# Second block of a fused network: a norm's residual rows in pieces on VectorE beside the next product, and the transposes of log f placed behind the products of q

## The chip, the cores and the metric

One core of a Trainium2 chip runs the whole program in one launch. The metric is device microseconds of that core. Before the change, three runs gave a median of 2824.99 us (2821.97 to 2828.13).

## The reference, cut to what matters

Two networks run one after the other on 256 tokens of width 1024, each with two layers. The first (an RWKV mixer with convolutions) ends in an RMS norm with the gain `final_g`. The second, which the change touches, is, per layer,

```python
x = layer_norm(ALPHA * x + 0.5 * swiglu_2(x, ffn1_w13[l], ffn1_w2[l]), ln_g[l, 0], ln_b[l, 0])
m = mixer(x, ...)
x = layer_norm(ALPHA * x + m, ln_g[l, 1], ln_b[l, 1])
x = layer_norm(ALPHA * x + 0.5 * swiglu_2(x, ffn2_w13[l], ffn2_w2[l]), ln_g[l, 2], ln_b[l, 2])
```

The mixer multiplies x by one wide matrix, whose parts are called q, f, i, g, u, v, a and b. From f it makes a gate and `log_f`, whose running sums give the decays of a recurrence (HGRN2); q reads the state of that recurrence. Everything is float32.

## The kernel before, in words

**Products.** Each float32 product is three matmuls: a weight tile of 128x1024 is split into a high half `wh` (a cast on ScalarE, L339) and a low half `wl` (raw minus high, on VectorE, L340), the moving operand likewise, and `mm3` adds high*high, high*low and low*high (L331). `stream` brings the tiles in order: a transfer by the SP queue into one of four `raw` buffers (L346), then the split into one of five slots for each half (second block). `up` makes one feature tile from eight such steps.

**Norms.** `ln` first adds the product's result to ALPHA*x (L1143), half by half, and takes its statistics; `ln_norm` writes the normalised rows `yb`. Then `feature_major` transposes `yb` on TensorE (L436), and ScalarE, VectorE and GpSimd take the result out of PSUM in a written-out order (`EVAC`), with gain and bias applied per feature: a scaled tile (L452 to L456), its high half (L458) and its low half (L460). That is `xf`, the operand of the next product. The first weight tiles behind it are held: the low halves of two of them are made on GpSimd (L363), the following ones on VectorE behind the last evacuation.

The next norm also needs the normalised rows times gain plus bias in row form, as its residual. So behind `feature_major` two rows come in by transfers (L1168), and GpSimd runs for each of the two row blocks a multiplication (L1162) and an addition (L1163) of 128x1024 each. There are five such norms in the second block: three in layer 0 and two in layer 1, whose third takes another path, straight to the output. And there is one more place, at the head of `second`, where the final RMS norm of the first network has a gain but no bias (L1536).

**The mixer's head.** `mixer` takes four weight tiles for f (`mf`), applies sigmoids (L1184, L1186), a scaling on VectorE (L1187 to L1189) and a logarithm (L1191, function Ln). Then `log f` is transposed on TensorE (L1196) into two PSUM tiles of the lane that the products use, and ScalarE copies them out (L1198). After that come the four tiles for q, copied out by L1204, and then, in the next stage, eight tiles `mt` for i and v. The transposed log f is first read in the stage after that, where `E` tiles of decays are made (L1243 on).

**What sets the order.** The program is traced in Python; a scheduler then simulates a timeline and orders each engine's instructions by program position among those that are ready, so an instruction may be moved ahead of earlier ones that still wait. `issue_after` adds an edge to the order of one engine. `tick` advances a background generator `self.bg` by one step: `ffn` calls it once for each of its 22 feature tiles. In the second block that generator is empty before the change.

Of the kernel before, what the change touches and what calls it, by code (L numbers as in the profile page):

```python
# [14 lines left out]
P = 128  # L15
# [14 lines left out]
NRAW, NW, NL = 4, 3, 2  # L30
NW2, NL2 = 2, 3
NFIRST = 2

NLAST = 2, 4

# [221 lines left out]
class Prog:  # L257
# [75 lines left out]
    def mm3(self, out, w, x, start, stop):  # L333
        self.mm(out, w[0], x[0], start, False)
        self.mm(out, w[0], x[1], False, False)
        self.mm(out, w[1], x[0], False, stop)

    def split(self, src, hi, lo):
        self.nc.scalar.copy(hi, src)  # L339
# [183 lines left out]
    def up(self, out, w, x, n=NF):  # L523

        for k in range(n):
            s = slice(k * P, k * P + P)
            self.mm3(out, (w[0][:, s], w[1][:, s]), x[k], k == 0, k == n - 1)

    def accs(self):
        return [[self.pacc(2 * b + h) for h in range(2)] for b in range(2)]  # L530
# [606 lines left out]
    def ln(self, x, acc, l, i):  # L1137

        nc = self.nc

        def pre(b, h):
            s = HALF[h]
            nc.vector.scalar_tensor_tensor(x[b][:, s], x[b][:, s], ALPHA, acc[b][h], ALU.mult, ALU.add)  # L1143

        g, bt = l * 3 + i, 6 + l * 3 + i
        if l == 1 and i == 2:
            gr, br = self.row(g), self.row(bt)
            for b in range(2):
                y = self.ln_norm(x[b], b, pre)
                for h in range(2):  # L1150
                    e = nc.vector if h == b else nc.gpsimd
                    e.tensor_mul(y[:, HALF[h]], y[:, HALF[h]], gr[:, HALF[h]])  # L1152
                    e.tensor_add(y[:, HALF[h]], y[:, HALF[h]], br[:, HALF[h]])  # L1153
                    nc.sync.dma_start(self.ap["out"][b * P : b * P + P, HALF[h]], y[:, HALF[h]])
            return None
        go, bo = COLS[f"lng{l}"][0] + i * 8, COLS[f"lnb{l}"][0] + i * 8
        yb = [self.ln_norm(x[b], b, pre) for b in range(2)]
        xf = self.feature_major(yb, lambda f: self.cols[:, go + f : go + f + 1],
                                lambda f: self.cols[:, bo + f : bo + f + 1])
        gr, br = self.row(g), self.row(bt)  # L1160
        for b in range(2):
            nc.gpsimd.tensor_mul(x[b], yb[b], gr)  # L1162
            nc.gpsimd.tensor_add(x[b], x[b], br)  # L1163
        return xf

    def row(self, i):
        r = self.S([P, D])
# [3 lines left out]
    def mixer(self, l, xf):  # L1171
# [17 lines left out]
                nc.vector.tensor_scalar(lf[:, h, :], sg, 1e-19, None, ALU.max)  # L1189
        for h2 in range(2):  # L1190
            nc.scalar.activation(lf[:, 2 * h2 : 2 * h2 + 2, :], lf[:, 2 * h2 : 2 * h2 + 2, :], AF.Ln)  # L1191
        lft = []
        for b in range(2):
            pt = self.ps((P, 4, P))
            for h in range(4):
                nc.tensor.transpose(pt[:, h, :], lf[:, h, b * P : b * P + P], self.cst("ident"))  # L1196
            t = self.T2([P, 4, P])
            nc.scalar.copy(t, pt)  # L1198
            lft.append(t)
        for h2 in range(2):  # L1200
            pu = self.ps((P, 2, T))
            for j in range(2):
                self.up(pu[:, j, :], next(st), xf)
            nc.scalar.copy(qs[:, 2 * h2 : 2 * h2 + 2, :], pu)  # L1204
        yield

        st = self.stream(f"mt{l}")
        it, vt = self.S([P, 2, 512]), self.S([P, 2, 512])
        for part in range(2):
            pb = [self.ps() for _ in range(2)]  # L1210
            for k2 in range(4):
                w = next(st)
                for kk in range(2):
                    k = k2 * 2 + kk
                    ws = [w[i][:, kk * 512 : kk * 512 + 512] for i in range(2)]
                    for b in range(2):
                        s = slice(b * P, b * P + P)
                        for a, c in ((0, 0), (0, 1), (1, 0)):
                            self.mm(pb[b], xf[k][a][:, s], ws[c], k == 0 and a == 0 and c == 0, k == 7 and a == 1)
            for b in range(2):  # L1220
                if part == 0:
                    nc.scalar.copy(it[:, b, :], pb[b])
                else:
                    nc.scalar.activation(vt[:, b, :], pb[b], AF.Gelu_apprx_tanh)
# [305 lines left out]
    def second(self):  # L1530
        nc = self.nc

        xf = self.feature_major(self.x, lambda f: self.col("fg", f), None)
        gr = self.row(12)
        for b in range(2):
            nc.gpsimd.tensor_mul(self.x[b], self.x[b], gr)  # L1536
        nc.sync.dma_start(self.h4T, self.ap["h4T"])
        mf = self.S([P, 7 * P])
        nc.sync.dma_start(mf, self.ap["msk"])
        nc.vector.tensor_copy(self.msk, mf)  # L1540
        nc.sync.dma_start(self.ind, self.ap["ind"])
        self.triu = self.ind[:, 8 * P : 9 * P]
        for l in range(2):
            acc = self.ffn(xf, f"pu{l}", f"pd{l}", 0.5)
            xf = self.ln(self.x, acc, l, 0)
            for _ in self.mixer(l, xf):
                pass
            acc = self.wout(self.mixed, f"mo{l}")
            xf = self.ln(self.x, acc, l, 1)
            acc = self.ffn(xf, f"qu{l}", f"qd{l}", 0.5)  # L1550
            xf = self.ln(self.x, acc, l, 2)
# [72 lines left out]
```

## Time and profile before

| | |
|---|---|
| median of 3 runs | 2824.99 us (2821.97 to 2828.13) |
| profiled execution, own time | 2827.67 us |
| its span | 2825.4 us, 53790 instructions |
| TensorE matmul (PE) busy | 2654.2 us, 94% |
| VectorE (DVE) busy | 1740.3 us, 62% |
| ScalarE (ACT) busy | 1332.7 us, 47% |
| GpSimd (POOL) busy | 734.4 us, 26% |
| second block | from about 1570 us to the end |

PE is the engine that matters: its matmuls fill nearly the whole span, so time goes where PE waits, or where its granted clock (PEclk, 1.00 is 2.4 GHz, 0.50 is 1.2 GHz) is at the lower level. The times in a timeline are microseconds from the start of the span; "idle before" names what the engine waited for.

### The profile page before, as it was taken

The numbers are of one execution on the slowest core, as the hardware profiler recorded it, in microseconds if no ns is written. First come the engines' busy times: TensorE is split into PE (matmuls) and PEld (weight loads), VectorE is DVE, ScalarE is ACT, GpSimd is POOL, SyncE is SP. The second block draws the span as 40 slices with busy tenths as digits, with TensorE's granted clock in tenths as the row PEclk, the third lists the DMA queues.
The fourth block names the chain that finished last, engine by engine and source line by source line (L and its number), as shares of the span: only waits on it lengthen the run. The fifth ranks groups of instructions, "written<-read, shape, count | busy, mean of one in ns | idle before, by whom it ended". The sixth has DMA issues, their size and how long they took to land. (4 is left out here: it accounts for less than half of the span.)

```text
span 2825.4 us, 53790 instructions
## 1 busy us (share of the span) xinstructions
PE 2654.2 (94%) x22398; PEld 2308.0 (82%) x22398; DVE 1740.3 (62%) x2659; ACT 1332.7 (47%) x2019; POOL 734.4 (26%) x691
## 2 busy tenths in 40 slices
PE   7889989999889998899899899899999999899998
PEld 4866867888578896766799899789899898789897
DVE  3875778654586556974555655665655655656655
ACT  5523654434564346433544544644444544644443
POOL 0387999920130002483100100200200201200200
PEclk8979999999999999979899999999999999999999
DMA  6344425334223453243455554524555554425553
GB/s 246 108 143 166 151 83 179 132 124 176 93 89 114 142 186 120 100 165 108 149 185 187 187 187 172 175 83 161 170 185 178 179 187 164 154 89 179 194 187 120
DMA packets 118768, 430.70 MB, mean 152 GB/s; under 512 B 13175, under 2 KB 13687, under 8 KB 118525
## 3 DMA queue, kind: packets, MB, share of 16 engines
q1 hardware_dynamic: 118524, 427.28, 43.6%
q8 instruction: 175, 2.87, 0.4%
q14 instruction: 69, 0.56, 0.1%
HBM read 425.13 MB, written 2.10 MB: 151 GB/s over the span
## 5 line engine op out<-in xcount | busy, mean ns | idle before, releaser
L340 DVE TENSOR_TENSOR wl<-raw,wh 128x1024 fp32r<-128x1024 f32 (+1 forms) x654 | 851.6, 1305 | 635.0 <-ACT wh L339 403.2
L339 ACT CAST wh<-raw 128x1024 fp32r<-128x1024 f32 (+1 forms) x654 | 682.3, 1046 | 902.1 <-PE pb L331 356.9
L331 PE MATMUL pb<-S,wh 128*128 128x256 f32 x2560 | 496.3, 291 | 7.6 <-DVE S L460 4.8
L331 PE MATMUL pb<-xf,wh 128*128 128x256 f32 (+1 forms) x2560 | 489.1, 290 | 12.9 <-DVE T1b L585 4.3
L331 PEld LDWEIGHTS pb<-xf,wh 128*128 128x128 f32 (+1 forms) x2560 | 412.5, 195 | 26.7 <-DVE T1b L585 7.8
L331 PEld LDWEIGHTS pb<-S,wh 128*128 128x128 f32 x2560 | 412.5, 194 | 24.5 <-issue 11.4
L331 PE MATMUL ps<-S,wh 128*128 128x256 f32 x2048 | 396.6, 290 | 5.2 <-DVE S L460 3.0
L363 POOL TENSOR_TENSOR wl<-raw,wh 128x1024 fp32r<-128x1024 f32 x22 | 54.8, 2499 | 1325.7 <-ACT wh L362 934.5
L331 PE MATMUL pb<-xf,wl 128*128 128x256 f32 (+1 forms) x1280 | 373.4, 292 | 8.9 <-DVE wl L340 8.9
L331 PE MATMUL pb<-S,wl 128*128 128x256 f32 x1280 | 370.0, 289 | 2.9 <-DVE wl L340 2.9
L331 PEld LDWEIGHTS ps<-S,wh 128*128 128x128 f32 x2048 | 331.9, 195 | 15.6 <-DVE S L460 4.3
L331 PE MATMUL ps<-S,wl 128*128 128x256 f32 x1024 | 296.3, 289 | 4.5 <-DVE wl L340 4.5
L331 PEld LDWEIGHTS pb<-xf,wl 128*128 128x128 f32 (+1 forms) x1280 | 250.3, 196 | 17.1 <-DVE wl L340 11.9
L331 PEld LDWEIGHTS pb<-S,wl 128*128 128x128 f32 x1280 | 248.0, 194 | 7.9 <-DVE wl L340 3.7
L331 PE MATMUL acc<-wh,T 128*128 128x512 f32 x704 | 206.4, 394 | 1.5 <-ACT T L339 1.5
L331 PEld LDWEIGHTS ps<-S,wl 128*128 128x128 f32 x1024 | 199.2, 195 | 6.8 <-DVE wl L340 4.9
L331 PE MATMUL acc<-wh,T1b 128*128 128x512 f32 x528 | 158.8, 399 | 3.5 <-ACT T1b L339 3.5
L729 POOL TENSOR_SCALAR tap<-z,cols 128x255 f32<-128x255 f32 (+14 forms) x120 | 154.6, 1297 | 0.0
L331 PEld LDWEIGHTS acc<-wh,T 128*128 128x128 f32 x704 | 127.3, 189 | 26.0 <-ACT T L339 1.9
L729 POOL TENSOR_SCALAR tap<-x,cols 128x246 f32<-128x246 f32 (+6 forms) x104 | 111.5, 1080 | 45.6 <-DVE x L668 45.5
L730 POOL TENSOR_TENSOR x<-x,tap 128x247 f32<-128x247 f32 (+8 forms) x132 | 105.3, 797 | 38.4 <-ACT tap L727 32.1
L331 PE MATMUL acc<-wl,T 128*128 128x512 f32 x352 | 113.2, 395 | 0.0
(448 smaller groups left out, 4025.5 us busy)
## 6 DMA issues: line engine op xcount, KB each, us to landing
raw<-in_fu SPq DMA_DIRECT2D x132, 512.0 KB, 3.2
raw<-in_ada SPq DMA_DIRECT2D x96, 512.0 KB, 4.1
raw<-in_pu SPq DMA_DIRECT2D x88, 512.0 KB, 3.9
raw<-in_qu SPq DMA_DIRECT2D x88, 512.0 KB, 4.2
raw<-in_fd SPq DMA_DIRECT2D x66, 512.0 KB, 3.2
raw<-in_wr SPq DMA_DIRECT2D x51, 512.0 KB, 3.6
raw<-in_pd SPq DMA_DIRECT2D x44, 512.0 KB, 3.5
raw<-in_qd SPq DMA_DIRECT2D x44, 512.0 KB, 3.6
```

Source lines behind the costliest of these rows:

```text
L331: return self.nc.tensor.matmul(out, lhsT, rhs, start=start, stop=stop, **kw)
L339: self.nc.scalar.copy(hi, src)
L340: self.nc.vector.tensor_sub(lo, src, hi.bitcast(F32))
L363: self.nc.gpsimd.tensor_sub(lo, r, hi.bitcast(F32))
L729: nc.gpsimd.tensor_scalar(t[:, d], z[:, f, s], w(j), None, ALU.mult)
L730: nc.gpsimd.tensor_add(zc[f][:, d], zc[f][:, d], t[:, d])
```

## The change

It has two parts. The residual rows leave GpSimd: a generator `affine` makes them on VectorE in pieces of 128x512, one per `tick`, after three empty ticks; `ffn` ticks once per feature tile, and the mixer's `mt` stage now ticks twice for each of its eight weight tiles. And the transposes of log f stand behind the last matmul of q, with PSUM tiles of another lane ("h", the four accumulator banks).

```diff
+NLATE = 3
...
     def mm3(self, out, w, x, start, stop):
...
-        self.mm(out, w[1], x[0], False, stop)
+        return self.mm(out, w[1], x[0], False, stop)
...
-        gr, br = self.row(g), self.row(bt)
-        for b in range(2):
-            nc.gpsimd.tensor_mul(x[b], yb[b], gr)
-            nc.gpsimd.tensor_add(x[b], x[b], br)
+        self.bg = self.affine(x, yb, self.row(g), self.row(bt))
         return xf
+
+    def affine(self, x, y, g, b=None):
+        nc = self.nc
+        for _ in range(NLATE):
+            yield
+        for i in range(2):
+            for s in HALF:
+                nc.vector.tensor_mul(x[i][:, s], y[i][:, s], g[:, s])
+                if b is not None:
+                    yield
+                    nc.vector.tensor_add(x[i][:, s], x[i][:, s], b[:, s])
+                yield
...
-        lft = []
-        for b in range(2):
-            pt = self.ps((P, 4, P))
-            for h in range(4):
-                nc.tensor.transpose(pt[:, h, :], lf[:, h, b * P : b * P + P], self.cst("ident"))
-            t = self.T2([P, 4, P])
-            nc.scalar.copy(t, pt)
-            lft.append(t)
         for h2 in range(2):
             pu = self.ps((P, 2, T))
             for j in range(2):
-                self.up(pu[:, j, :], next(st), xf)
+                last = self.up(pu[:, j, :], next(st), xf)
             nc.scalar.copy(qs[:, 2 * h2 : 2 * h2 + 2, :], pu)
+        lft = []
+        with self.tc.issue_after(last.ins):
+            for b in range(2):
+                pt = self.ps((P, 4, P), "h")
+                for h in range(4):
+                    nc.tensor.transpose(pt[:, h, :], lf[:, h, b * P : b * P + P], self.cst("ident"))
+                t = self.T2([P, 4, P])
+                nc.scalar.copy(t, pt)
+                lft.append(t)
         yield
...
             for k2 in range(4):
+                self.tick()
+                self.tick()
                 w = next(st)
...
-        gr = self.row(12)
-        for b in range(2):
-            nc.gpsimd.tensor_mul(self.x[b], self.x[b], gr)
+        self.bg = self.affine(self.x, self.x, self.row(12))
```

## Rows read from the trace of the kernel before

**Rows 1.** Busy time by stretch: feed-forward, then `mt`; PE, PEld, DVE, ACT, POOL, PEclk, DMA
```profile
1600.00:1755.00 155.00, 155.00 (x1111) 146.35 (x1110) 79.82 (x93) 68.57 (x93) 0.00 (x0) 1.00 0.56 190
...
1805.00:1828.00 23.00, 23.00 (x100) 18.39 (x99) 11.00 (x10) 12.43 (x15) 0.00 (x0) 1.00 0.54 186
```

**Rows 2.** Waits of PE in the second block (1570 to 2825): total us, times, longest
```profile
PE acc L436 <- DVE S L404: 8.2, 5, 1.6
...
PE ps L331 <- DVE wl L340: 4.5, 2, 2.3
PE pb L1196 <- ACT S L1191: 3.9, 1, 3.9
PE ps L331 <- DVE S L460: 3.0, 2, 1.8
PE pb L331 <- DVE S L460: 2.9, 2, 1.8
PE pb L331 <- DVE wl L340: 2.9, 3, 2.3
PE ps L1196 <- ACT S L1191: 2.7, 1, 2.7
PE acc L331 <- ACT T L339: 1.5, 2, 1.3
```

**Rows 3.** POOL's groups by line, the whole span: count, busy us, mean ns
```profile
L1163 POOL TENSOR_TENSOR x<-x,S 128x1024 f32<-128x1024 f32 x10 | 33.5, 3368 | 0.0
...
L1162 POOL TENSOR_TENSOR x<-S,S 128x1024 f32<-128x1024 f32 x10 | 25.4, 2562 | 0.0
```

**Rows 4.** POOL's timeline at the first norm of layer 0: start, us
```profile
1775.11 5.07 POOL L1162 TENSOR_TENSOR x<-S,S 128x1024 f32<-128x1024 f32 x2
```

**Rows 5.** DVE's timeline at the same norm and behind it
```profile
1771.95 1.10 DVE L460 TENSOR_TENSOR S<-T,S 128x256 fp32r<-128x256 f32 x3
...
1774.68 3.27 DVE L460 TENSOR_TENSOR S<-T,S 128x256 fp32r<-128x256 f32 x2 [0.72 <-ACT S L458]
1777.88 11.19 DVE L340 TENSOR_TENSOR wl<-raw,wh 128x1024 fp32r<-128x1024 f32 x4
...
1790.36 1.21 DVE L340 TENSOR_TENSOR wl<-raw,wh 128x1024 fp32r<-128x1024 f32 x1
...
1805.63 0.69 DVE L1311 TENSOR_TENSOR T<-T,ind 128x512 f32<-128x512 f32 x1 [1.23 <-DMA T<-in_sgws]
```

**Rows 6.** Busy time and granted clock in short stretches at the five norms (columns as in rows 1)
```profile
1771.00:1776.00 5.00, 4.07 (x22) 3.06 (x22) 4.20 (x9) 4.91 (x13) 2.31 (x3) 1.00 0.50 185
1778.00:1783.80 5.80, 5.79 (x27) 5.79 (x28) 5.80 (x2) 2.33 (x2) 5.80 (x3) 0.50 0.26 85
2007.70:2012.80 5.10, 5.10 (x24) 5.10 (x25) 5.10 (x2) 0.26 (x1) 5.10 (x2) 0.50 0.47 157
2197.10:2200.40 3.30, 3.30 (x18) 3.30 (x18) 2.55 (x7) 3.24 (x10) 1.42 (x2) 0.51 0.50 187
2207.30:2210.80 3.50, 3.50 (x19) 3.50 (x18) 3.50 (x2) 0.88 (x1) 3.50 (x2) 0.51 0.45 150
2394.90:2398.50 3.60, 3.53 (x14) 3.15 (x15) 2.86 (x8) 3.50 (x10) 1.01 (x2) 0.53 0.62 245
2401.90:2405.40 3.50, 3.50 (x17) 3.50 (x18) 3.50 (x2) 2.33 (x2) 3.50 (x2) 0.51 0.00 0
2416.30:2419.00 2.70, 2.70 (x13) 2.70 (x14) 1.73 (x3) 2.67 (x4) 0.00 (x0) 0.50 0.78 228
2630.70:2634.00 3.30, 3.30 (x18) 3.30 (x16) 3.30 (x2) 0.00 (x0) 3.30 (x2) 0.50 0.46 166
```

**Rows 7.** PE's timeline at that norm: the last matmul of f
```profile
1789.53 0.28 PE L331 MATMUL pb<-S,wl 128*128 128x256 f32 x1
```

**Rows 8.** ACT's timeline there: the second logarithm
```profile
1798.32 0.63 ACT L1191 ACTIVATE S<-S 128x512 f32<-128x512 f32 x1
```

**Rows 9.** SP's queue at that norm: when the two rows are asked for
```profile
1768.53 0.90 SPq L1168 DMA_DIRECT2D S<-in_rows  x2
```

More of the change, by code (lines that the diff above doesn't have):

```diff
@@ L526, in up @@
             s = slice(k * P, k * P + P)
-            self.mm3(out, (w[0][:, s], w[1][:, s]), x[k], k == 0, k == n - 1)
+            last = self.mm3(out, (w[0][:, s], w[1][:, s]), x[k], k == 0, k == n - 1)
+        return last
     def accs(self):
```

## The prediction

> **What bounds the kernel now.** I read the busy time by stretch first. In the feed-forward parts and in the mixer's `mt` stage PE is busy for the whole stretch, at the full granted clock, while DVE is busy 79.8 of 155 us and 11.0 of 23 us [rows 1]. So in these stages PE sets the pace and DVE has about half of its time free. What can be won or lost lies where PE waits, and I read the list of its waits next [rows 2]. There I see four kinds that bear on the change: for the last evacuations of a norm (`S L460`), for low halves of weights (`wl L340`), for log f (`S L1191`), and for a product's own halves (`T L339`).
>
> The timelines say why the first two are late. POOL begins its four row operations at 1775.11 [rows 4], with means of 2.56 and 3.37 us for the multiplication and the addition [rows 3]: 2 x 2.56 + 2 x 3.37 = 11.9 us, so to about 1787. DVE needs 1.10 us for three evacuations before that, 0.37 each; the last two take 3.27 us together, and then four weight splits take 11.19 us, 2.80 each, where one after POOL's end takes 1.21 [rows 5]. Both engines read two SBUF operands; while they run together DVE is slowed more than twofold. The reader is to see that POOL's work, which nothing waits for, sits at the one place in which DVE is PE's supplier.
>
> The third thing is the clock. Right behind these gaps the granted clock is at 0.50 for 5.8, 5.1, 3.5, 3.5 and 3.3 us, at all five norms, and for 2.7 us behind the longer wait for log f [rows 6].
>
> **The change part by part.** The sum goes against the profiled execution, 2827.67 us for a span of 2825.4; that is 2.7 us above the median, so I take the gain off the median, 2824.99.
>
> *POOL's rows gone.* DVE then makes the last two evacuations in 2 x 0.37 = 0.7 us in place of 3.27, and each split in 1.21 in place of 2.80 [rows 5]. At the first norm the last evacuation would come at 1774.68 + 0.74 = 1775.4 instead of 1777.95; PE stood still from about 1776.2 (its wait of 1.8 us ends at 1778.0 [rows 2, 6]), so the wait goes, with 0.8 us to spare. The first DVE-made weight would be ready at 1776.6. It is wanted when the first two weights are through: 27 matmuls were still to run at 1778.0 [rows 6], 3.1 us at the full rate from 1776.2, so at 1779.3: 2.7 us to spare. The waits that go are 3.0 + 2.9 us for evacuations (four) and 4.5 + 2.9 us for low halves (five), 13.3 us; the 1.5 us for a product's halves go too, since they queue on DVE behind the same splits [rows 2]. Sum 14.8 us.
>
> *The clock behind those gaps.* At 0.50, 27 matmuls of 256 columns took 5.8 us, 0.215 each [rows 6]; in the `mt` stage 100 of 512 columns took 23 us, 0.115 for 256 [rows 1]. So 1 - 0.115 / 0.215 = 46% of a slow stretch is lost: 0.46 x (5.8 + 5.1 + 3.5 + 3.5 + 3.3) = 9.8 us, if the clock no longer falls.
>
> It may still fall. The norm leaves gaps of its own (`S L404`, 8.2 us in five waits [rows 2]), and at two norms the clock was low before POOL's work mattered, from 2197.1 and from 2394.9; at the first norm it was full between 1771 and 1776, so there these gaps had not lowered it [rows 6]. From the two in five I expect about one further fall: 0.46 x 3.3 = 1.5 us given back. At worst all three norms that were spared fall, 4.6 us. The Trainium skill, "TensorE: Matmul & The Clock Gate", part 1 (the HAM clock gate), says that the gate watches activity in windows that run free of the kernel, so the same gap may lower the clock in one place and not in another. By that rule the two in five are a matter of phase and are drawn anew after the change; with all three falling the sum would be 3 us lower than mine. The trace agrees so far as like norms differ.
>
> *The transposes.* PE waits 3.9 and 2.7 us for log f at the head of the two mixers [rows 2], and the stretch of 2.7 us at the low clock behind the longer one costs 0.46 x 2.7 = 1.2 us: together 7.8 us. With q's products next, PE goes straight on: its weights lie ready, since their splits follow the four of the 11.19 us, which shrink to 4.8. The eight transposes take the same PE time wherever they stand. What is late next is log f itself: its second logarithm ends 9.2 us after PE's last matmul of f (1798.95 against 1789.8 [rows 7, 8]); q's four tiles are 4 x 24 matmuls of 0.115, 11.0 us. So the transposes find it ready with 1.8 us to spare, and a miss would cost little more than a microsecond in each mixer; if the cover were wholly gone, it would be the old 6.6 us. The copies out of PSUM stay on ACT, twice per mixer, and their reader is a whole stage of 23 us away. The PSUM lane "h" is empty then, as the norm's evacuation is over. I take the gain of 7.8 whole.
>
> *The pieces on DVE.* Five norms with 8 pieces and one with 4 make 44. The nearest row is a 128x512 product of two SBUF tiles, 0.69 us [rows 5]: 44 x 0.69 = 30.4 us of DVE. In the feed-forward part one comes per tile, and DVE is half idle; in `mt` eight come in about 12 us beside splits of 1.21 per 2.9 us, which raises DVE from 48% to (11.0 + 5.5) / 23 = 72%. The cover is this idle time and the split slots ahead of PE, so the price is nothing as long as the pieces lie there. But the scheduler moves ready work forward: a mixer constant that the program asks for two stages later was made at 1805.63, in the middle of q's and `mt`'s work [rows 5]. A piece may so slip in between evacuations or splits, where it costs 0.69 less the slack worked out above. Bounds: 0, and 8 x 0.69 = 5.5 us a norm; I take 0.5 us at each of the six places, 3.0 in all, nearer to nothing because of the slack of 0.8 and 2.7 us.
>
> *The other queues.* SP asks for the same two rows at the same point (1768.53 [rows 9]), and they had landed when POOL began at 1775.11 [rows 4]; no transfer is added. DVE, not POOL, now waits for them: behind it queue the splits. POOL has nothing behind its rows before the next norm.
>
> Sum: 14.8 + 9.8 + 7.8 - 1.5 - 3.0 = 27.9 us; 2824.99 - 27.9 = 2797.1.
>
> **The rivals.** *A: the clock goes on falling at every norm*, because the norm's own gaps suffice. For it: 2197.1 and 2394.9. Against: the full clock at the first norm. If each fall were as long as now, the 9.8 us stay, the 1.5 of my forecast is counted in them: 14.8 + 7.8 - 3.0 = 19.6, giving 2805.4.
>
> *B: the pieces slip ahead of the splits.* All eight before the first low half cost 5.5 - 2.7 = 2.8 us at each of five norms, 14 us, and the gaps so made lower the clock as now: 9.8 - 1.5 = 8.3 more than I allow. 27.9 + 3.0 - 14 - 8.3 = 8.6, giving 2816.4. For it: the early constant. Against: three empty ticks, and splits stand earlier in the program.
>
> *C: slower.* A piece stands in DVE's queue ahead of the evacuations and waits there for its row. The rows may land as late as 1775.1 while the evacuations run from about 1770.2: up to 5 us with DVE blocked, then 5.5 us of pieces, 10.5 a norm in place of a lost 3 (14.8 / 5). Five norms: 7.5 x 5 = 37 us more than now, less the transposes' 7.8: 2854. It decides from about 4.6 us lost per norm. Against it: evacuations come first in the program.
>
> *D: the transposes don't get away*, because log f comes as late after q as it did before. 27.9 - 6.6 - 1.2 = 20.1, giving 2804.9. Against it: the 1.8 us of slack.
>
> **How the numbers follow.** Forecast 0.70, A 0.13, B 0.08, C 0.03, D 0.06. The predicted time is the forecast's, 2797. The range reaches down to all gains with no give-back, 27.9 + 4.5 = 32.4, so 2792.6, with 1.6 for the spread of the runs: 2791; and up to A and D at 2805, with another 4 for both at once in part: 2809. B and C are left out. A measurement can tell about 0.2%, 5.6 us: forecast, A, D and most of B are faster than that, 0.92; the rest of B and a milder C lie within it, 0.05; C slower, 0.03.
>
> **What would show it.** POOL should show no 128x1024 rows behind norms. DVE's splits there should take 1.2 us each; PE's waits for `S L460` and `wl L340` should be gone, and no wait of the transposes should appear before `mt`. The 44 pieces should take some 0.6 to 0.7 us and lie beside a PE that is busy throughout. Wrong would be: PE waits for DVE of more than a microsecond in the first 20 us behind a norm, pieces among the evacuations, or a low clock at all five norms without any long gap.

## The result, and the profile after

| | before | after |
|---|---|---|
| median of the runs on one chip | 2826.56 us (2821.97 to 2830.82, 4 runs) | 2786.38 us (2783.58 to 2793.36, 4 runs) |
| ratio, 95% interval | | 0.9862 (0.9837 to 0.9887) |
| profiled execution | 2827.67 us | 2783.58 us |

The change saves 40 us, where 28 were predicted; 2786.4 lies below the low end of the range, 2791. The direction and the mechanism held, the size was too small.

The busy time of the engines on the page after the change (the line with the span, then the engines):

```profile
span 2781.8 us, 53780 instructions
...
PE 2632.1 (95%) x22398; PEld 2291.3 (82%) x22398; DVE 1716.4 (62%) x2703; ACT 1327.3 (48%) x2015; POOL 670.2 (24%) x669
```

POOL has lost 64 us, and DVE, which took over the work, is no busier than it was: the 30 us of pieces cost it less than the slowed splits had. The waits of PE in the second block, total us, times, longest, against [rows 2]:

```profile
PE acc L438 <- DVE S L406: 8.2, 5, 1.6
PE acc L438 <- ACT x L423: 7.0, 1, 7.0
PE acc L333 <- ACT E L1261: 5.9, 4, 2.0
PE pb L333 <- DVE wl L342: 2.0, 2, 1.1
PE ps L333 <- DVE wl L342: 0.6, 1, 0.6
```

Gone are the waits for the last evacuations by DVE, for a product's own halves and for log f; of the 7.4 us for low halves 2.6 are left. DVE's timeline at the first norm of layer 0 says what those are (start, us; against [rows 5]):

```profile
1764.07 1.09 DVE L462 TENSOR_TENSOR S<-T,S 128x256 fp32r<-128x256 f32 x2 [0.72 <-ACT S L460]
1765.33 1.23 DVE L342 TENSOR_TENSOR wl<-raw,wh 128x1024 fp32r<-128x1024 f32 x1 [0.17 <-ACT wh L341]
1766.47 2.49 DVE L1174 TENSOR_TENSOR x<-S,S 128x512 f32<-128x512 f32 x4
1768.88 2.35 DVE L342 TENSOR_TENSOR wl<-raw,wh 128x1024 fp32r<-128x1024 f32 x2
```

The last two evacuations take 1.09 us in place of 3.27, a split 1.2 in place of 2.80. But four pieces stand right behind the first split: the three empty ticks place them later in the program, and the scheduler takes them as soon as they are ready. There are 44 pieces, as planned, of 0.68 us each on average.

The granted clock (the third number from the end, columns as in [rows 1]) in stretches around a norm where it fell, and at one where it did not:

```profile
1758.00:1764.00 6.00, 4.64 (x22) 3.93 (x23) 4.59 (x11) 4.50 (x13) 0.92 (x2) 0.72 0.71 264
...
1970.00:1976.00 6.00, 3.89 (x27) 2.79 (x25) 4.89 (x12) 3.37 (x9) 1.54 (x1) 1.00 0.56 216
```

A mean of 0.72 over 6 us is 3.4 us at 0.50. The norms at 2166, 2360 and 2578 read 0.72 as well, so in this execution the clock still falls at four of the five norms, but for 4 x 3.4 = 13.6 us in all, where [rows 6] list 28.1 us at or behind the five. (In the repeat of the kernel after, below, it falls at three of them, again for 13.6 us.) The falls behind a norm's last evacuations are what vanished.

**Where the time is counted.** PE runs the same 14204 matmuls in the first block before and after, and yet single executions of all kernels spent between 1555 and 1576 us in it. So I compare the second block: from the first weight split that is held behind the last norm of the first network, to the end of the span. It took 1259.1 us before and 1225.1 after.

### The profile page after: what moved, and what is told of

Read it like the earlier page. It is cut to its first block, busy times and chain, and to the rows that moved or that the text cites. A ratio compares the mean times of both kernels' runs of the same rounds, so it can differ in the third digit from the quotient of the medians.

```text
span 2781.8 us, 53780 instructions
## 1 busy us (share of the span) xinstructions
PE 2632.1 (95%) x22398; PEld 2291.3 (82%) x22398; DVE 1716.4 (62%) x2703; ACT 1327.3 (48%) x2015; POOL 670.2 (24%) x669
## 4 chain that ended last, share of the span: by engine, by line
PE 78%; DVE 11%; ACT 4%; POOL 3%; issue 2%; DMA 2%; SPq 0%; ACTq 0%; DVEq 0%; POOLq 0%
PE pb L333 33%; PE acc L333 25%; PE ps L333 19%; DVE wl L342 3%; DVE T1c L726 1%; POOL tap L732 1%; DVE S L964 1%; DVE T L962 1%; DMA raw<-in_ada 1%; DVE x L621 1%; ACT wh L341 1%; POOL x L733 1%; PE acc L438 1%; DMA raw<-in_wr 0%; DVE T2b L620 0%
## 5 line engine op out<-in xcount | busy, mean ns | idle before, releaser
L342 DVE TENSOR_TENSOR wl<-raw,wh 128x1024 fp32r<-128x1024 f32 (+1 forms) x654 | 811.9, 1245 | 622.2 <-ACT wh L341 391.7
L333 PE MATMUL ps<-S,wh 128*128 128x256 f32 x2048 | 390.4, 287 | 0.6 <-ACT S L460 0.5
L733 POOL TENSOR_TENSOR z<-z,tap 128x255 f32<-128x255 f32 (+14 forms) x120 | 112.8, 940 | 3.9
```

Of the source, the lines that this page charges most:

```text
L333: return self.nc.tensor.matmul(out, lhsT, rhs, start=start, stop=stop, **kw)
L342: self.nc.vector.tensor_sub(lo, src, hi.bitcast(F32))
L733: nc.gpsimd.tensor_add(zc[f][:, d], zc[f][:, d], t[:, d])
```

## The experiments

All of them in one table. The ratio is to the kernel before, from runs on the same chip; the second block is that of one profiled execution. Two of the kernels, "rows left out" and "full rows", leave a part of the computation out.

| kernel | median us | ratio, 95% | second block us |
|---|---|---|---|
| before, again | 2824.5 | 1.000 (0.9989 to 1.0011) | 1262.5 |
| change, again | 2783.2 | 0.9861 (0.9842 to 0.9881) | 1222.5 |
| rows alone | 2798.9 | 0.9917 (0.9904 to 0.9930) | 1239.8 |
| transposes alone | 2808.7 | 0.9954 (0.9939 to 0.9968) | 1253.3 |
| rows left out | 2781.5 | 0.9854 (0.9839 to 0.9868) | 1223.2 |
| pieces tied | 2783.0 | 0.9855 (0.9834 to 0.9876) | 1219.6 |
| rows late on GpSimd | 2783.1 | 0.9853 (0.9835 to 0.9871) | 1217.6 |
| multiplications three times | 2788.6 | 0.9866 (0.9845 to 0.9887) | 1224.9 |
| norms filled | 2790.3 | 0.9876 (0.9852 to 0.9901) | 1225.6 |
| rows alone, log f filled | 2792.8 | 0.9875 (0.9849 to 0.9901) | 1230.0 |
| tied and filled | 2781.5 | 0.9849 (0.9822 to 0.9876) | 1217.2 |
| full rows | 2772.9 | 0.9830 (0.9814 to 0.9847) | 1210.5 |
| padded rows | 2776.0 | 0.9817 (0.9801 to 0.9832) | 1211.0 |
| tied and padded | 2770.5 | 0.9796 (0.9782 to 0.9809) | 1209.6 |

### Both kernels again

The kernel after, unaltered.

> The changed kernel again, unaltered. In the first profiles its first block took 1556.7 us against 1566.3 us before, with the same order of instructions there, and its second block 1225.1 against 1259.1. Theory 'chance': the 9.6 us of the first block are the granted clock of single executions, so this profile's first block lies anywhere from 1556 to 1570, not tied to the kernel, and the whole gain over many runs is about 34, a ratio near 0.988. Rival 'first block too': something of the change reaches the first block, so it stays at 1555 to 1559 in every kernel that carries the change, and the ratio stays at 0.9855 or less. In both the second block is 1225, give or take 4.

The gain came back: 2783.2 against 2823.3 us, ratio 0.9861. The 40 us are no accident of the first runs. The first block took 1555.3 us, which both readings allow; the next run decides between them. The kernel before, unaltered, with a profile of its own:

> The kernel before, unaltered, with a profile of its own: is its first block (the same order of instructions in every kernel here) really slower? Its first profile had 1566.3 us there with 208 us at the lower clock; five profiles with the change or a part of it had 1555.3 to 1560.7 with 184 to 188. Theory 'chance': a new profile lies anywhere, as likely as not near 1556 to 1561. Rival 'first block too': again 1563 to 1569 and over 200 us at the lower clock. The second block is 1259, give or take 4, in both; ratio 1.000.

Of the stretch before the second block, the window view gives, for this execution of the kernel before (columns as in [rows 1]; then the two stretches behind the waits for log f):

```profile
0.00:1555.00 1555.00, 1441.27 (x14203) 1195.69 (x14204) 999.69 (x1655) 728.83 (x1182) 606.13 (x633) 0.94 0.43 144
1781.61:1786.50 4.89, 4.89 (x23) 4.89 (x24) 3.31 (x8) 3.37 (x6) 0.00 (x0) 0.50 0.94 304
2406.15:2411.10 4.95, 4.95 (x23) 4.95 (x24) 3.31 (x8) 3.38 (x6) 0.00 (x0) 0.50 0.87 271
```

Its first block is as short as that of the kernel after, at 0.94 of the full clock. So the 10 us by which the first two profiles differ there were a matter of the single execution, and the change gains nothing in the first block. Its second block is as long as before, 1262.5 us. And it shows something that the first profile did not: the waits for log f on PE's timeline (the bracket is the idle time before) are longer,

```profile
1781.61 0.69 PE L1196 MATMUL ps<-const,S 128*128 128x128 f32 x2 [4.96 <-ACT S L1191]
...
2406.15 0.69 PE L1196 MATMUL pb<-const,S 128*128 128x128 f32 x2 [4.97 <-ACT S L1191]
```

9.9 us together where [rows 2] have 6.6, and behind each of them the clock is at the lower level for 4.9 us, where [rows 6] have one such stretch of 2.7.

### One part alone

The rows as in the change, the transposes in their old place and lane:

```diff
+        lft = []
+        for b in range(2):
+            pt = self.ps((P, 4, P))
...
-        with self.tc.issue_after(last.ins):
```

> Only the rows move to VectorE; the transposes of log f stand at their old place. Theory 'supplier' (the rows on GpSimd slowed VectorE while it fed TensorE): waits for evacuations and low halves (13.3) and 1.5 more go, with the slow clock behind them (9.8): second block 1259.1 - 24.6 + 2.6 (three small waits for low halves that the pieces cause) = 1237, and TensorE waits for log f again, 4 to 7 us in two waits. Rival 'transposes do the most': no more than 12 us, second block 1247 or more. Ratio 0.991 to 0.993 by the first, 0.995 or more by the second.

2798.9 us, ratio 0.9917: 0.0083 of 2824.5, so 23.4 us less than before, as the reading 'supplier' had it. The list of PE's waits has the log f line grown, not unchanged,

```profile
PE ps L1210 <- ACT S L1205: 7.2, 1, 7.2
...
PE pb L1210 <- ACT S L1205: 6.0, 1, 6.0
```

13.2 us where 4 to 7 were expected, and behind the two waits PE works without a pause at the lower clock for 2.9 and 5.7 us:

```profile
1781.89:1784.80 2.91, 2.91 (x14) 2.91 (x15) 0.00 (x0) 0.46 (x1) 0.00 (x0) 0.50 0.75 231
2393.50:2399.20 5.70, 5.70 (x28) 5.70 (x28) 0.27 (x2) 0.70 (x2) 0.00 (x0) 0.50 0.71 274
```

When PE no longer waits at the norm it comes to log f earlier, and log f does not come earlier by as much: in the mixers the rows alone gain only 2.4 us each (from the transposes of one norm to those of the next), the rest is passed on to the next wait. The reverse, the transposes moved and the rows on GpSimd as before:

```diff
-        self.bg = self.affine(x, yb, self.row(g), self.row(bt))
+        gr, br = self.row(g), self.row(bt)
+        for b in range(2):
+            nc.gpsimd.tensor_mul(x[b], yb[b], gr)
+            nc.gpsimd.tensor_add(x[b], x[b], br)
```

> Only the transposes move; the rows stay on GpSimd. Theory 'supplier': the two waits for log f (6.6) and one slow stretch (1.2) go, the waits of the norms stay: second block 1259.1 - 7.8 = 1251, ratio 0.997. Rival: with VectorE still slowed by the rows, q's weights come late and give half of it back: 1255.

2808.7 us, ratio 0.9954 (0.9939 to 0.9968): 13.0 us less than before, between 9 and 17, reckoned likewise, and more than either reading expected. The second block of the one profiled execution is only 7.5 us shorter (1253.3 against 1260.8, the mean of the two profiles of the kernel before), so for this kernel the many runs and the one profile disagree. The waits of PE for DVE at the norms are back,

```profile
PE ps L333 <- DVE wl L342: 5.5, 6, 2.3
...
PE ps L333 <- DVE S L462: 2.2, 3, 1.1
```

and none for log f is in the list. By the ratios the parts nearly add up: 23.4 + 13.0 = 36.4 of the change's 39.3. In the profiles they do not: the second block is 21.0 us shorter with the rows alone, 7.5 with the transposes alone, and 37.0 with both (1223.8, the mean of the two profiles of the change). So the transposes are worth more with the rows moved than without: 0.9917 - 0.9861 = 0.0056 of 2824.5, 15.8 us, and 1239.8 - 1223.8 = 16.0 us of the second block.

### What the pieces cost

First the work left out altogether (two transfers stay).

```diff
-        self.bg = self.affine(x, yb, self.row(g), self.row(bt))
+        self.row(g), self.row(bt)
```

> The changed kernel without the 44 pieces: the rows are brought in, but gain and bias are not applied to the residual (this part of the computation is left out). Theory 'pieces cost a little': the three waits of 0.6, 1.1 and 0.9 us for low halves behind the norms before feed-forward parts go: second block 2 to 3 us less than in the changed kernel beside it, some more if the clock falls less. Rival 'pieces are free': the same within 1 us, waits for low halves still there.

2781.5 us, ratio 0.9854: the 30 us of VectorE work cost nothing that these runs can tell, and the three waits for low halves are gone. Then the pieces tied to their place, each behind the gating product of the feature tile of its tick:

```diff
+            self.dve = nc.vector.scalar_tensor_tensor(s, pu, half, s, ALU.mult, ALU.mult)
...
+                with self.pin():
+                    nc.vector.tensor_mul(x[i][:, s], y[i][:, s], g[:, s])
```

> The changed kernel with each piece in the feed-forward parts tied behind VectorE's product of the tile before (an edge in VectorE's order), so the pieces really stand one per feature tile from the fourth on; in the mixers nothing is altered. Theory 'the pieces are paid where they stand among the first weight splits': the waits of 0.6, 1.1 and 0.9 us for low halves go, three feed-forward stretches take 0.5 to 1.5 us less each, and no wait appears later: second block 1220 to 1223, 2 to 3 us under the changed kernel. Rival 'late pieces cost too': TensorE waits for a product's halves or for low halves in mid-stretch, second block 1225 or more.

Ratio 0.9855: the waits for low halves are gone, and the second block is 2.9 and 5.5 us shorter than in the two profiles of the change, but the interval of the ratio holds the change's. The same rows on GpSimd, but after a gate that opens three ticks later:

```diff
+        gate = nc.gpsimd.tensor_copy(self.lt("T1", [P, T], lane="r"), self.made)
...
+                with self.tc.issue_after(gate.ins):
+                    nc.gpsimd.tensor_mul(x[i][:, s], y[i][:, s], g[:, s])
```

> The rows stay on GpSimd, in pieces of 128x512, but start only behind the third feature tile (or, in the mixers, behind the copy of q): a small GpSimd copy of that tile stands ahead of them. Transposes as in the change. Theory 'place, not engine': in the feed-forward parts VectorE is half idle and TensorE has weights ahead, so VectorE's slowing by some 9 us a norm is taken up: second block 1222 to 1232, and no wait for S L460. Rival 'the shared reading hurts anywhere': VectorE falls behind there as well, low halves come late, second block 1240 or more.

Ratio 0.9853, as good as the change. POOL's timeline in the second feed-forward part:

```profile
2007.23 7.21 POOL L1177 TENSOR_TENSOR x<-S,S 128x512 f32<-128x512 f32 x4
```

and DVE's beside it:

```profile
2010.98 2.31 DVE L342 TENSOR_TENSOR wl<-raw,wh 128x1024 fp32r<-128x1024 f32 x1
```

DVE is slowed here too, 2.3 us for a split that takes 1.2 alone, and no wait of PE comes of it. What did the harm was the place of the rows, not the engine. And the multiplications done three times over, 16 pieces at each of the five norms in place of 8:

```diff
-                nc.vector.tensor_mul(x[i][:, s], y[i][:, s], g[:, s])
+                for _ in range(3 if b is not None else 1):
+                    nc.vector.tensor_mul(x[i][:, s], y[i][:, s], g[:, s])
```

> The changed kernel with every multiplication at the five norms done three times (16 pieces a norm in place of 8; the result is the same). Theory 'slack of 2 to 3 us, then paid': the added 5.5 us of VectorE come among the first splits too; low halves come late by 3 to 5 us at each of the three norms before feed-forward parts, less in the mixers, and the clock falls behind some: second block 1225 + 9 to 22. Rival 'hidden': VectorE's idle half takes them, within 3 us of the changed kernel.

Ratio 0.9866, the waits for low halves are 2.0 us, where the change has 2.6. The reading that they would queue ahead of the splits was a miss. DVE's timeline at the second norm says why:

```profile
1987.59 2.49 DVE L1175 TENSOR_TENSOR x<-S,S 128x512 f32<-128x512 f32 x4
1990.00 2.35 DVE L342 TENSOR_TENSOR wl<-raw,wh 128x1024 fp32r<-128x1024 f32 x2
1992.27 1.28 DVE L1175 TENSOR_TENSOR x<-S,S 128x512 f32<-128x512 f32 x2
```

Four go first, as in the change, then splits take their turn again, and every further piece lies between splits that are in time.

### What the clock costs

Products without use, to keep TensorE at work through the gaps: ten repeated transposes in each norm,

```diff
+            if self.tags is TAGS2 and acc and (f, b) == (NF - 1, 0):
+                for k in range(10):
+                    nc.tensor.transpose(pt[k % 4][:, 1, 0, :], yb[0][:, (2 * (k % 4) + 1) * P : (2 * (k % 4) + 2) * P], self.cst("ident"))
```

> The changed kernel with ten transposes of a norm's first row block done twice, behind the first eight: about 1.4 us of TensorE work laid into the gap of 1.6 us in which it waits for the second row block (S L406), at the head and at all five norms. Theory 'the falls of the clock that are left at the norms come from this gap': 10 to 14 us at the lower clock there go, some 4 to 6 us: second block near 1219. Rival 'the added transposes only lie in the gap': the same falls, second block 1222 to 1226.

The falls at the norms are gone, all 13.6 us of them; the second block is not shorter, 1225.6 us, and the ratio 0.9876 is no better. A miss. The same stretch behind the wait of the first norm, in the change and then in this run, shows that PE gets no further at the full clock (103 matmuls in 15.24 us, PEclk 0.89 and 1.00),

```profile
1758.88:1774.12 15.24, 14.65 (x103) 13.74 (x104) 13.71 (x23) 12.64 (x23) 1.46 (x2) 0.89 0.55 191
...
1766.28:1781.52 15.24, 13.91 (x103) 12.63 (x104) 13.71 (x23) 12.56 (x23) 1.46 (x2) 1.00 0.53 184
```

and the waits of PE tell why:

```profile
PE acc L438 <- DVE S L406: 4.3, 5, 0.9
PE ps L333 <- ACT S L463: 1.4, 3, 0.5
...
PE ps L333 <- POOL S L465: 0.7, 2, 0.4
```

At the full clock PE comes sooner to halves that ScalarE and GpSimd have not made yet. In these stretches the evacuations set the pace, and a low clock costs little or nothing: 3.4 us of it cost nothing at the norms before the mixers, and 0.3 to 0.4 us at the other two. At the head of the block, where PE has no gap for them, the ten added transposes cost 1.3 us, which takes up what the norms gained. The other place, 32 transposes of a constant ahead of those of log f, on the kernel with the rows alone:

```diff
+            if b == 0:
+                with self.tc.issue_after(lastf.ins):
+                    for k in range(32):
+                        nc.tensor.transpose(pt[:, k % 4, :], self.cst("ident"), self.cst("ident"))
```

> Rows on VectorE, the transposes of log f at their old place, and between the last product of f and these transposes 32 transposes of a constant tile, about 4.4 us of TensorE work laid into the wait for log f (7.2 and 6.0 us in the run with the rows alone, second block 1239.8, 13.6 us at the lower clock right behind the two waits). Theory 'the wait for log f costs its length and then a fall of the clock': the end of the wait stays where it is, the falls behind it go: 0.46 x 13.6 = 6 us less, second block 1234, still about 10 over the whole change. Rival 'the clock there has another cause': 1238 or more.

1230.0 us for the second block against 1239.8 without the fill, and the ratio is better as well, 0.9875 against 0.9917. But the run is not the test that it was meant to be. PE's timeline in the first mixer:

```profile
1782.76 3.66 PE L1212 MATMUL ps<-const 128*128 128x128 f32 x32
1786.17 0.48 PE L333 MATMUL ps<-S,wh 128*128 128x256 f32 x2
...
1792.23 0.44 PE L1214 MATMUL ps<-const,S 128*128 128x128 f32 x2
```

Behind the 32 added transposes PE does not wait for log f: it goes on with the products of q (the line at 1786.17), and log f is transposed 6 us later, among them. The order changed, and no wait for log f is left in the list of PE's waits. So two things went at once. The two waits of 13.2 us made room for 2 x 3.4 us of useless work, 6.4 us less; and the 8.6 us at the lower clock behind them (the 13.6 of the expectation lay in part inside the waits) went, an estimated 0.46 x 8.6 = 4.0 us. The sum, 10.4 us, is near the 9.8 that came back, but the run does not part the one from the other. That the low clock costs time behind this wait is seen in the run with the rows alone, where PE works through both stretches at 0.50 without a pause. Both fills with the tied pieces, and 40 more transposes at the head of the block:

```diff
+        if bias is None:
+            for k in range(40):
+                nc.tensor.transpose(pt[k % 4][:, 0, 0, :], self.cst("ident"), self.cst("ident"))
```

(with the edits of the tied pieces and of the filled norms)

> A version meant to beat the changed kernel: pieces tied to their feature tiles, the norms' gaps filled as in the run before the last, and 40 transposes of a constant tile in the 7.0 us for which TensorE waits at the head of the second block (x L423), so that the clock does not fall there (6.8 us low behind it so far). By the theory that falls follow idle gaps: 1219.6 - 3 (head) - 3 to 5 (norms) = 1212 to 1214 for the second block, ratio to the kernel before 0.981 to 0.983. Rival: falls come all the same, 1219 and 0.985.

PE's waits fall to 16.6 us and the low clock of the second block to 20 us, and the ratio, 0.9849, is not distinguishable from that of the tied pieces alone. Measured by its expectation, a miss too.

### What is left in the mixer

The longest low stretch that remains in the first profile of the change, 10.2 us, lies in the later part of a mixer, where PE does not wait. Two kinds of products stand there that use few rows of the array: a bias as a product with one row, and a factor per head with four. (The trace shows each of these float32 products as two matmuls: the sixteen that the next expectation counts are the matmuls of eight products in each mixer.) First both replaced by products of full height (the bias and the factor are left out):

```diff
-                self.mm(pm[:, j, :], self.h4T[0:4, h * P : h * P + P], r4)
+                self.mm(pm[:, j, :], self.cst("ident"), os_[:, h, :])
...
-                    self.mm(pm[:, j, b, :], self.cst("ones")[0:1, :], bs[0:1, g * P : g * P + P], False, True)
+                    self.mm(pm[:, j, b, :], self.cst("ident"), ws[:, g, :], False, True)
```

> The changed kernel, where in each mixer sixteen products with one row of contraction (a bias through a row of ones) and the four with four rows (a norm's factor spread to 128 rows) get a 128-row constant as the other operand: the same columns, but the bias and that norm's factor are left out of the computation. In every profile so far, of both kernels, the clock falls once per mixer for 3.4 to 10.2 us right behind this stretch, though TensorE never waits there. Theory 'the clock falls behind products with few rows': both falls go, second block 2 to 5 us less, 1219 to 1222 (changed kernel: 1225.1 and 1222.5). Rival 'it falls for another reason, or by its own rhythm': falls stay, 1222 to 1226.

Then the same products as in the change, with their operands widened to 128 rows by zeros:

```diff
-        bs = self.T2([1, 512])
-        nc.sync.dma_start(bs, self.ap["sgbs"][l])
+        bs = self.T2([P, 512])
+        nc.gpsimd.memset(bs, 0.0)
+        nc.sync.dma_start(bs[0:1], self.ap["sgbs"][l])
...
-                self.mm(pm[:, j, :], self.h4T[0:4, h * P : h * P + P], r4)
+                self.mm(pm[:, j, :], self.h4T[:, h * P : h * P + P], r4)
```

> The changed kernel with the same 20 products a mixer, whose second operands are padded with zero rows to 128 rows of contraction (computation kept). Theory 'products with few rows cost twice: each takes longer, and the clock falls behind them': the stretch from the gate's bias step to the next norm takes 140 to 143 us in both mixers (145.3 to 149.8 in the changed kernel, 140.6 with the norm's factor left out), no fall of the clock in it, second block 1211 to 1215, ratio 0.982 to 0.984. Rival 'it was the wait for the norm's factor that went': 145 to 148 and second block 1221 or more, ratio 0.986.

And the padded rows with the tied pieces:

```diff
+                with self.pin():
+                    nc.vector.tensor_mul(x[i][:, s], y[i][:, s], g[:, s])
...
+                self.mm(pm[:, j, :], self.h4T[:, h * P : h * P + P], r4)
```

> Padded rows and the pieces tied to their feature tiles: by the same theory 2 to 3 us under the run before it in the second block, 1209 to 1212, with no wait of TensorE for low halves behind the norms. Rival: the tied pieces bring nothing, the same within 1 us.

Ratios 0.9830, 0.9817 and 0.9796 (0.9782 to 0.9809). The last is the best of the study: its interval lies wholly below the change's and it leaves nothing out, so it beats both kernels. What the tied pieces add there, 1.4 us of the second block, lies between its two readings. In all three the part of the mixer from its first GpSimd multiplication to the next norm's first held split takes 140.6 or 140.7 us, where it took 145 to 150 in the profiles of the change, and no fall of the clock lies in it: the reading that products with few rows cost twice held. POOL's timeline has both ends, first in the change, then in the run with the padded rows:

```profile
1814.87 1.26 POOL L1336 TENSOR_TENSOR S<-S,T 128x512 f32<-128x512 f32 x1 [50.32 <-DVE S L1335]
...
1960.13 2.40 POOL L365 TENSOR_TENSOR wl<-raw,wh 128x1024 fp32r<-128x1024 f32 x1 [131.45 <-ACT wh L364]
...
1816.20 1.26 POOL L1340 TENSOR_TENSOR S<-S,T 128x512 f32<-128x512 f32 x1 [49.85 <-DVE S L1339]
...
1956.92 2.40 POOL L365 TENSOR_TENSOR wl<-raw,wh 128x1024 fp32r<-128x1024 f32 x1 [126.66 <-ACT wh L364]
```

More rows on these products stand in the last section.

## Why the prediction was too small

**What bounds the kernel: right.** PE sets the pace, and what was won lay in its waits and in the clock behind them. PE's waits in the second block went from 45.5 to 25.4 us, or 46.6 to 25.4 in the repeats. The time at the lower clock, summed over the block's stretches, fell from 71.8 and 79.0 us to 44.9 and 38.9, by 33.5 on average; at 46% lost that is 15.4, a rough figure, since a fall inside a norm costs less. Together 20.6 + 15.4 = 36 us, and the second block is 37.0 shorter (1260.8 against 1223.8, means of two). The medians give 39 to 40; the last 2 or 3 us are within what one execution differs from the next. And 3.2 of the 37.0 us are not the change's doing: they lie in the later part of the two mixers (296.8 us before, 293.6 after, means of two), where no instruction of the change stands and the length of the falls differs from one execution to the next.

**POOL's rows gone: right.** Splits at 1.2 us, as the sum had them, the last two evacuations in 1.09 us where it had 0.7, and the waits for `S L460` of DVE and the product's halves gone. By the ratio the rows alone gain 23.4 us (20 to 27) against 14.8 + 9.8 - 1.5 - 3.0 = 20.1 in the sum: inside the interval.

**The pieces: the price right, the place wrong.** I took 3.0 us; the three waits for low halves that are left make 2.6, and the tied pieces remove them. But the sentence that put the pieces beside a busy PE had them held back by the empty ticks, and four stand right behind the first split of each norm. That is the placement of rival B in part. It did not cost 14 us: the first split still goes ahead, and the four take 2.49 us, about the 2.7 us of slack that the working had found. A part of rival B's condition came true and its price did not. With three times the multiplications no more than four go ahead, so no run shows what all eight ahead of the first split would cost.

**The clock behind the norms: the count about right, the price too high.** I expected two falls of five to stay and one to be added. Four are there in the first profile of the change and three in its repeat, so the count is a matter of the single execution, and rival A's five came in neither. But the sum priced a fall at 0.46 of its length, and the filled norms showed that removing all 13.6 us gives next to nothing back, because the evacuations feed PE no faster there. The reserve of 1.5 us was hardly called. The Trainium skill, "TensorE: Matmul & The Clock Gate", part 1 (the HAM clock gate), says that the gate's windows run free of the kernel, and that the same kernel therefore shows different numbers of slow matmuls from run to run. The traces agree: the same 14204 matmuls of the first block took from 1555 to 1576 us, with 174 to 222 us of them at the lower clock.

**The transposes: the step that failed.** "together 7.8 us" took 3.9 and 2.7 us of waiting and one low stretch of 2.7 us from a single execution of the kernel before, and added them to a sum in which the norms' waits ahead of them are gone. The mechanism was right: the second logarithm ended at 1784.46 + 0.63 = 1785.09, in ScalarE's timeline after the change,

```profile
1784.46 0.63 ACT L1205 ACTIVATE S<-S 128x512 f32<-128x512 f32 x1
```

and PE's transposes followed at 1786.12 without a wait,

```profile
1786.12 0.60 PE L1216 MATMUL acc<-const,S 128*128 128x128 f32 x4
```

so rival D fell, with 1.0 us to spare in place of 1.8. The size was off, for two reasons. One execution was not enough: in the repeat of the kernel before, the same two waits were 9.9 us and the clock lay low for 4.9 us behind each, 9.9 + 2 x 0.46 x 4.9 = 14.4 in place of 7.8. And the two parts were priced apart: without the norm's waits PE comes to log f sooner and waits longer there. The run with the rows alone shows it, 13.2 us of waits and 8.6 us at the lower clock behind them, 13.2 + 0.46 x 8.6 = 17.2. That is what the transposes take away inside the change, and there they were measured at 15.8 us by the ratios and 16.0 in the second block, twice the term.

The range failed with it: its low end allowed for "no give-back", but the term's bound was only a lower one (the old wait if the cover were gone). The sum fell 11.4 us short of the 39.3 by the ratios. With the rows first and the transposes on top of them, 3.3 lie in the rows' term, which their interval covers, and 15.8 - 7.8 = 8.0 in the transposes'. In the other order 5.2 lie in the transposes' and 6.2 in the rows'; the shares depend on the order because the two parts work on waits that follow each other. In either order the transposes' term is the one that its interval excludes.

**Rival C: fell.** No piece stands in front of an evacuation, and none waited for its row there.

What stays open: how much of the rows' 23 us is wait and how much clock, since the two cannot be taken apart by runs that differ by a few microseconds; why the clock falls at some norms and not at others, and not at the same ones in the next execution; and why the one profile of the transposes alone gained 7.5 us where its runs gained 13.0.

## What to carry to other kernels

Work that nobody waits for can still do harm where it runs beside the one moment in which another engine is the supplier; move it by a few microseconds before you move it to another engine. A wait that is removed is worth its own length, plus the low clock behind it where TensorE sets the pace, and little or nothing for the clock where its feed does; and a wait that follows close behind grows by part of what the first one gave up, so price the two together. Take the length of such waits, and the clock behind them, from more than one profiled execution, and let the range reach to the longest. When work without use is put into a gap, look whether the order around it stayed the same before reading its time.

## What the runs showed of the hardware

Products that use one row or four rows of the array were costlier than their size. After the change the one-row products alternate with full ones; each float32 product shows as two matmuls, here in PE's groups over the whole span (count of matmuls, busy us, mean ns):

```profile
L333 PE MATMUL acc<-T,const 1*128 1x128 f32 x32 | 7.7, 321 | 0.0
...
L333 PE MATMUL acc<-T,h4T 4*128 4x256 f32 x16 | 5.8, 517 | 0.0
```

On PE's timeline in the first mixer, at the full granted clock, each product, a pair of matmuls, takes 0.42 us, 0.21 for one matmul, the full ones between them too:

```profile
1881.01 0.48 PE L333 MATMUL acc<-T,const 1*128 1x128 f32 x2
1881.42 0.49 PE L333 MATMUL acc<-T,S 128*128 128x128 f32 x2
...
1884.23 1.99 PE L333 MATMUL acc<-T,h4T 4*128 4x256 f32 x8
```

Behind them the clock falls, though PE was busy for the whole time (busy time in these stretches, columns as in [rows 1]; the last is the same place in the second mixer):

```profile
1881.00:1884.20 3.20, 3.20 (x16) 2.25 (x15) 2.00 (x3) 3.17 (x4) 0.00 (x0) 1.00 0.10 13
1884.20:1886.10 1.90, 1.90 (x9) 1.40 (x8) 1.21 (x2) 0.67 (x2) 0.00 (x0) 1.00 0.69 254
1886.10:1890.20 4.10, 4.10 (x23) 4.05 (x23) 3.48 (x7) 0.62 (x1) 0.00 (x0) 0.60 0.02 6
...
2488.00:2498.40 10.40, 10.40 (x42) 9.14 (x42) 5.04 (x10) 2.82 (x5) 0.00 (x0) 0.52 0.12 44
```

With the operands padded by zeros to 128 rows, PE's timeline of that kernel has the same pairs at 0.22 us each, 0.11 for one matmul,

```profile
1881.10 0.39 PE L333 MATMUL acc<-T,const 128*128 128x128 f32 x2
1881.32 0.39 PE L333 MATMUL acc<-T,S 128*128 128x128 f32 x2
...
1882.78 1.89 PE L333 MATMUL acc<-T,h4T 128*128 128x256 f32 x8
```

and the window view the full clock throughout:

```profile
1872.00:1882.00 10.00, 10.00 (x81) 8.89 (x80) 3.40 (x3) 5.16 (x7) 0.00 (x0) 1.00 0.30 105
1882.00:1892.00 10.00, 10.00 (x80) 9.79 (x79) 8.85 (x15) 6.74 (x10) 0.00 (x0) 1.00 0.29 93
```

The eight four-row matmuls take about as long at either height (1.99 and 1.89 us); the longer mean of the narrow ones in the list is that of the second mixer, where they fell into the low clock. Both kinds were widened together, so which of them brings the clock down is open.
